# A new order for the head of a decoder step: normalization, transposes, splits, first weights

## The chip, the cores and the metric

The kernel runs on one core of a Trainium2 chip. The metric is the time of one execution in microseconds (us) of device time, as the median of several runs. The engines are PE (TensorE, matmuls and transposes), DVE (VectorE), ACT (ScalarE), POOL (GpSimd) and SP (SyncE, which issues the transfers here). PSUM is the memory that PE writes, in 8 banks; SBUF is the memory that all engines work from.

## The reference

One layer of a decoder trunk for a prompt of 1024 tokens and a sample group of 8 x 8 tokens, which share the weights:

```
h = rmsnorm(x, norm_pre)                      # per token over D_MODEL = 1024
proj = h @ w_in                               # (tokens, 1024) x (1024, 5648)
z, xBC, dt, u, g, gates = split(proj)
branch A: causal conv of width 4 on xBC, SiLU, SSD scan in chunks of 128,
          D skip, SiLU(z) gate, grouped rmsnorm, @ w_branch_a
branch B: trailing means of u (windows 2, 4, 8, 16) minus u, per-group map,
          scale, SiLU(g) gate, @ w_branch_b
merged = sigmoid(gate_a) * A + sigmoid(gate_b) * B
y = x + rmsnorm(merged @ w_out, norm_post)
```

It also returns the convolution, SSD and pool states of both groups. All is float32.

## The kernel before

**Tiles.** The 1088 tokens are nine tiles: tiles 0 to 7 of 128 prompt tokens, tile 8 with the 64 sample tokens. The head normalizes each tile, transposes it (so that channels lie on the partitions) and splits it into a rounded high part `Hhi` and a rest `Hlo` (1024 x 1088 each). Each projection is made of groups of 24 matmuls (`group3`, L142): for one block of 128 output channels and one of three token ranges (256, 384 and 448 columns: tiles 0 and 1, tiles 2 to 4, tiles 5 to 8), eight blocks of input channels times three products (high x high, low x high, high x low). A block of weights (`Slab`) is loaded (L120) and split in the same way into `whi` (a cast on ACT, L93) and `wlo` (a subtraction, L94).

**Order.** Nothing is scheduled automatically: the order in which the program is written is the order of each engine's queue. `main` is the list of matmul groups; a slot is one of its places, and `at_pe(slot, ...)` puts work ahead of that slot's group, `at(slot, ..., key)` behind it, in the order of the keys. The first six groups are the weight blocks 0 and 1 in turn over the three token ranges, so the first group needs tiles 0 and 1 and weight block 0, the second the same tiles and block 1, the third and fourth also tiles 2 to 4, the fifth and sixth also tiles 5 to 8.

**The head's steps.** The head is written as a string of two-character steps, a letter and a tile number; its first part runs ahead of the first group, and the parts behind a bar ahead of the second to fifth group. `loads` is a second such string, for the transfers on SP's queue. The letters:

- R: broadcast half of `norm_pre` to all partitions by a matmul (L1122), and copy it (DVE, L1123).
- N: square and sum of one tile (ACT, L200), then two tiny POOL operations that make the reciprocal root (L182, L183).
- S, D: the tile times root times `norm_pre` (DVE, L209), as one instruction (S) or two halves (D).
- T, U: four transposes each on PE (L223), channels 0 to 511 and 512 to 1023, into one PSUM bank of tag "xb", "pyo" or "pst" by the tile number modulo 3. Each tag has two banks.
- E, F: split of what T or U wrote: the cast to `Hhi` (ACT, L93) and the subtraction to `Hlo` (DVE, L94).
- W, V: split of a weight block, the cast on ACT (L93), the subtraction on POOL (W) or on DVE (V), L94.
- H: a matmul of the identity that nothing reads (L1118). K: seven small POOL operations that make constants (L250 to L258). P: a transpose of the convolution parameters into a "pst" bank (L282) and two copies (L283, L284).
- In the string of transfers: X loads a tile, W a weight block, Q four small parameter tensors.

`hist_dma` loads the convolution history in two transfers (L272) into buffers that the normalized tiles use too (tag "xn", four of them), then the skip vector (L274), `dt_bias` (L277) and `a_log` (L278); `dts.load` follows (L371). ACT takes the exponential of `a_log` (L292) behind the fifth group. The convolution of a finished group runs behind the next groups: a copy out of PSUM and a scaling (ACT, L333 and L341), three taps (DVE, L347).

Of the kernel before, what the change touches and what calls it, by code (L numbers as in the profile page):

```python
# [37 lines left out]
def hybrid_decoder_step(  # L38
# [62 lines left out]
    def at(slot, fn, *args, key=1):  # L101
        post[slot].append((key, len(post[slot]), fn, args))
# [146 lines left out]
    def consts():  # L249
        nc.gpsimd.affine_select(tri, ones, [[1, 128]], ALU.is_ge, 0.0, base=0, channel_multiplier=-1)  # L250
        nc.gpsimd.memset(bones, 0.0)
        b64 = bones[0:64, 0:64].rearrange("p (b t) -> p b t", t=8)
        o64 = ones[0:64, 0:64].rearrange("p (b t) -> p b t", t=8)
        nc.gpsimd.affine_select(b64, o64, [[-8, 8], [0, 8]], ALU.is_ge, 0.0, base=0, channel_multiplier=1)
        nc.gpsimd.affine_select(b64, b64, [[8, 8], [0, 8]], ALU.is_ge, 0.0, base=7, channel_multiplier=-1)
        nc.gpsimd.memset(btri, 0.0)
        nc.gpsimd.tensor_tensor(btri[0:64, 0:64], bones[0:64, 0:64], tri[0:64, 0:64], op=ALU.mult)
        nc.gpsimd.tensor_copy(bm, b64[:, :, 0])  # L258
# [3 lines left out]
    def params_dma():  # L262
        prow = pbox["p"] = mt([72, 128])
        nc.sync.dma_start(prow[0:48], conv_w[0].rearrange("k (t p) -> (k t) p", p=128))
        nc.sync.dma_start(prow[48:60], conv_b[0].rearrange("(t p) -> t p", p=128))
        nc.sync.dma_start(prow[60:68], ssm_norm[0].rearrange("(t p) -> t p", p=128))
        nc.sync.dma_start(prow[68:72], pool_scale[0].rearrange("(t p) -> t p", p=128))
# [12 lines left out]
    def params_T():  # L280
        ps = bank("pst")
        nc.tensor.transpose(ps[:, 0:72], pbox["p"], ident[0:72, 0:72])  # L282
        nc.vector.tensor_scalar(par[:, 0:60], ps[:, 0:60], 0.5, None, op0=ALU.mult)  # L283
        nc.vector.tensor_copy(par[:, 60:72], ps[:, 60:72])  # L284
# [815 lines left out]
    def msplit(m):  # L1100
        mhl[m] = hi, lo = zt((128, LP), F32R), zt((128, LP), F32R)
        for h, l, v in ((hi, lo, mg[m][:, 0:LP]), (ms[m][:, 0:NS], ms[m][:, NS:128], mg[m][:, LP:LT])):
# [8 lines left out]
    nc.sync.dma_start(nrow, norm_pre)  # L1111
    loads = {"W": lambda i: cv[i].slab.dma(raw1[:, 0:1024].rearrange("p (k e) -> p k e", k=8) if i else None),
             "X": load_x, "Q": lambda i: params_dma()}
    for w in "X0 X1 X2 X3 W0 Q0 X4 W1 X5 X6 X7 X8".split():
        loads[w[0]](int(w[1]))

    def H(i):
# [2 lines left out]
    def R(e):  # L1120
# [3 lines left out]

    steps.update({"H": H, "R": R, "W": lambda i: cv[i].slab.conv(nc.gpsimd), "V": lambda i: cv[i].slab.conv(nc.vector),
                  "P": lambda i: params_T(), "K": lambda i: consts()})
    plan = ("R0 N0 R1 H0 N1 D0 H0 T0 U0 S1 N2 H0 S2 T1 N3 U2 T2 F0 W0 S3 E0 U1 E1 H0 T3 H0 U3 N4 F1 D4 W1 | "
            "T4 E2 E3 F2 N5 E4 N6 S5 P0 S6 F3 U4 F4 | "
            "U5 T5 | "
            "T6 N7 F5 K0 U6 D7 T7 E5 | "  # L1130
            "N8 S8 T8 U7 E7 U8 E6 E8 F6 F8 F7")
    for slot, part in enumerate(plan.split("|")):
        for w in part.split():
            fn, n = steps[w[0]], int(w[1])
# [10 lines left out]
    dts = DtStep()  # L1145
    at(3, dts.load, key=5)
    at(6, dts.conv, key=5)
    at(2, hist_dma, key=5)
    at(5, zfree, npre, key=9)

    for i in (8, 10, 2, 3):
# [318 lines left out]
```

## Time and profile before

| what | value |
|---|---|
| median of 3 runs | 913.35 us (912.92 to 913.99) |
| the profiled execution's own time | 914.17 us |
| its span | 912.5 us |
| PE busy | 897.1 us (98%), 5580 matmuls |
| DVE, ACT, POOL busy | 549.1, 346.0, 237.8 us |
| first L142 matmul | 18.43 us from the span's start |

The views in order of time give, for each engine, the start of an instruction in us from the span's start, its length, its line, what it writes and reads, its shape, and in brackets the idle time ahead of it with what ended it. Instructions of one kind that follow each other may stand in one row with their count. A PE row's length reaches to the end of its last matmul, which overlaps the next row; the distance between two starts is what an instruction takes of the engine.

### The profile page before, as it was taken

The page shows a single profiled execution, that of the slowest core. Times are in us where ns is not written, and L with a number is a line of the kernel's source. Part 1 is how long each engine was busy: PE and PEld are TensorE (multiplying, and loading weights), DVE is VectorE, ACT ScalarE, POOL GpSimd, SP SyncE. Part 2 cuts the span into 40 slices and gives each one's busy share as a digit, 9 for nine tenths or more (in the row PEclk, how much of TensorE's full clock was granted, in tenths as well). Part 3 has the DMA queues.
Part 4 walks back from the last instruction along what each step waited for, and adds up shares of the span by engine and source line. Part 5 has one row for each costly group of instructions (what it writes and reads, how often), then busy time and mean ns, then how long its engine had stood idle before and what let it go on. Part 6 is the DMA issues. An engine that isn't in the chain of part 4 may idle for free.

```text
span 912.5 us, 14410 instructions
## 1 busy us (share of the span) xinstructions
PE 897.1 (98%) x5580; PEld 830.8 (91%) x5580; DVE 549.1 (60%) x961; ACT 346.0 (38%) x762; POOL 237.8 (26%) x313
## 2 busy tenths in 40 slices
PE   8999989999999999999999999999999999999997
PEld 6999989999999999998999999999999999988886
DVE  6866797989776675456544353449356526972322
ACT  6645555656375452425343042111333223331111
POOL 6332354656465463121100000000000002510101
PEclk9999999999999999999999999999999999999999
DMA  8011323242335435454311233442121113632222
GB/s 270 8 47 37 85 76 112 68 131 59 107 99 164 120 88 152 116 162 116 93 37 36 35 109 109 148 136 76 54 56 34 45 54 123 228 113 73 92 97 89
DMA packets 112525, 87.97 MB, mean 96 GB/s; under 512 B 10694, under 2 KB 99754, under 8 KB 112457
## 3 DMA queue, kind: packets, MB, share of 16 engines
q1 hardware_dynamic: 112313, 86.92, 32.3%
q8 instruction: 44, 0.72, 0.4%
q14 instruction: 24, 0.20, 0.1%
q10 hardware_dynamic: 144, 0.13, 0.0%
HBM read 69.46 MB, written 17.56 MB: 95 GB/s over the span
## 4 chain that ended last, share of the span: by engine, by line
PE 67%; DVE 2%; DMA 2%; issue 1%; ACT 0%; POOLq 0%; POOL 0%; SPq 0%; DVEq 0%; ACTq 0%
PE m L142 34%; PE pyo L142 16%; PE m L1359 3%; PE pyo L1359 3%; PE xb L1359 3%; PE pst L1359 2%; DMA raw<-in_w_branch_a_dram 1%; PE pyo L568 1%; PE pyo L571 1%; PE xb L694 1%; DVE wlo L94 1%; PE pst L575 1%; PE pst L739 1%; DVE r L347 1%; PE pyo L735 1%
## 5 line engine op out<-in xcount | busy, mean ns | idle before, releaser
L142 PE MATMUL m<-Hhi,whi 128*128 128x384 f32 (+2 forms) x872 | 291.4, 334 | 0.6 <-ACT g L889 0.6
L142 PE MATMUL m<-Hhi,wlo 128*128 128x384 f32 (+2 forms) x872 | 287.1, 329 | 0.0
L142 PE MATMUL m<-Hlo,whi 128*128 128x384 f32 (+2 forms) x872 | 287.0, 329 | 0.0
L142 PEld LDWEIGHTS m<-Hhi,whi 128*128 128x128 f32 x872 | 166.0, 190 | 5.6 <-ACT g L889 1.1
L142 PEld LDWEIGHTS m<-Hlo,whi 128*128 128x128 f32 x872 | 165.9, 190 | 4.3
L142 PEld LDWEIGHTS m<-Hhi,wlo 128*128 128x128 f32 x872 | 165.6, 190 | 4.4
L347 DVE SCALAR_TENSOR_TENSOR r<-r,par,r 128x256 f32<-128x256 f32 (+2 forms) x108 | 97.2, 900 | 2.6
L93 ACT CAST whi<-raw 128x1024 fp32r<-128x1024 f32 (+1 forms) x67 | 59.7, 891 | 99.2 <-PE m L142 35.9
L94 DVE TENSOR_TENSOR wlo<-raw,whi 128x512 fp32r<-128x512 f32 (+1 forms) x46 | 46.7, 1015 | 84.1 <-ACT whi L93 83.9
L94 POOL TENSOR_TENSOR wlo<-raw,whi 128x1024 fp32r<-128x1024 f32 x21 | 51.5, 2452 | 39.9 <-ACT whi L93 34.3
L142 PE MATMUL pyo<-Hhi,whi 128*128 128x448 f32 (+2 forms) x184 | 60.3, 328 | 0.0
L142 PE MATMUL pyo<-Hhi,wlo 128*128 128x448 f32 (+2 forms) x184 | 60.3, 327 | 0.0
L142 PE MATMUL pyo<-Hlo,whi 128*128 128x448 f32 (+2 forms) x184 | 60.2, 327 | 0.0
L142 PE MATMUL m<-z,whi 128*128 128x256 f32 (+2 forms) x217 | 53.3, 327 | 0.0
L142 PE MATMUL pyo<-z,whi 128*128 128x384 f32 (+2 forms) x191 | 48.0, 332 | 1.2 <-ACT whi L93 1.2
L560 POOL TENSOR_TENSOR sa<-sa,cb 128x512 f32<-128x512 f32 x28 | 39.0, 1394 | 6.8 <-ACT sa L556 6.8
L142 PEld LDWEIGHTS m<-z,whi 128*128 128x128 f32 x217 | 38.0, 189 | 1.4
L598 DVE SCALAR_TENSOR_TENSOR z<-z,dsk,se 128x128 f32<-128x128 f32 x56 | 38.5, 727 | 1.0
L142 PE MATMUL m<-z,wlo 128*128 128x256 f32 (+2 forms) x115 | 37.5, 327 | 0.0
L94 POOL TENSOR_TENSOR wolo<-r,wohi 128x512 fp32r<-128x512 f32 x16 | 22.7, 1435 | 56.5 <-ACT wohi L93 53.2
L555 ACT ACTIVATE sa<-sa,acm 128x128 f32<-128x128 f32 x112 | 35.7, 392 | 2.7 <-DMA sa<-dscr 2.7
L341 ACT ACTIVATE r<-r,par 128x256 f32<-128x256 f32 (+2 forms) x36 | 25.1, 698 | 29.7 <-POOL r L329 16.6
(379 smaller groups left out, 1617.6 us busy)
## 6 DMA issues: line engine op xcount, KB each, us to landing
raw<-in_w_in_dram SPq DMA_DIRECT2D x43, 512.0 KB, 4.0
z<-in_x_prompt_dram SPq DMA_DIRECT2D x15, 512.0 KB, 5.2
sa<-dscr SPq DMA_DIRECT2D x28, 256.0 KB, 4.6
z<-spill SPq DMA_DIRECT2D x11, 544.0 KB, 5.4
raw<-in_w_branch_a_dram SPq DMA_DIRECT2D x16, 256.0 KB, 2.8
r<-in_w_out_dram SPq DMA_DIRECT2D x16, 256.0 KB, 4.4
se<-dscr SPq DMA_DIRECT2D x56, 64.0 KB, 4.0
out_dram<-q SPq DMA_DIRECT2D x14, 256.0 KB, 2.1
```

Source lines behind the costliest of these rows:

```text
L93: nc.scalar.copy(hi, src)
L94: (eng or nc.vector).tensor_tensor(lo, src, hi.bitcast(F32), op=ALU.subtract)
L142: nc.tensor.matmul(ps[:, 0:b - a], slab.w(k, p), rhs(k, p)[:, a:b], start=k == 0 and p == 0, stop=k == slab.kn - 1 and p == 2)
L341: nc.scalar.activation(A, R[:, 0:w], AF.Identity, bias=cb(i), scale=cw(0, i))
L347: nc.vector.scalar_tensor_tensor(A, R[:, k:k + w], cw(k, i), A, op0=ALU.mult, op1=ALU.add)
L555: nc.scalar.activation(A[:, h], A[:, h], AF.Relu, bias=acm[:, self.c, hh:hh + 1], scale=-1.0)
L560: nc.gpsimd.tensor_tensor(A, A, CBs[self.c, self.g].unsqueeze(1).to_broadcast([128, 4, 128]), op=ALU.mult)
L568: nc.tensor.matmul(py[64 * q:64 * q + 64, 128 * i:128 * i + 128], x0[:, 2 * i + q], A[:, 2 * i + q], start=True, stop=True)
L571: nc.tensor.matmul(py[:, 256 + 128 * i:384 + 128 * i], hs[:, 128 * i:128 * i + 128], Ct[self.g][:, self.cols], start=True, stop=True)
L575: nc.tensor.matmul(self.ps[:, 0:256], B[:, a], self.xx[:, b].rearrange("p h q -> p (h q)"), start=i == 0, stop=i == 2)
L598: nc.vector.scalar_tensor_tensor(xv, xv, dsk[:, j:j + 1], self.E[:, i] if self.c else py[:, 128 * i:128 * i + 128], op0=ALU.mult, op1=ALU.add)
L1359: nc.tensor.matmul(box["ps"][:, 0:b - a], lh, rh[k][:, a:b], start=kk == 0 and i == 0, stop=kk == 7 and rh is Wlo)
```

## The change

The two strings are written anew, and `hist_dma` moves from behind the third group to behind the fourth, ahead of `dts.load`. In the new string the first weight block is split by V0 (subtraction on DVE) where it was W0 (on POOL); K0 and P0 stand ahead of the first group, where K0 stood ahead of the fourth and P0 ahead of the second; W1 stands ahead of the second group; E0 stands ahead of N2; the scalings of tiles 5 to 8 are halves throughout; X4 is loaded ahead of Q0.

```diff
--- before.py
+++ after.py
@@ -1111,7 +1111,7 @@
     nc.sync.dma_start(nrow, norm_pre)
     loads = {"W": lambda i: cv[i].slab.dma(raw1[:, 0:1024].rearrange("p (k e) -> p k e", k=8) if i else None),
              "X": load_x, "Q": lambda i: params_dma()}
-    for w in "X0 X1 X2 X3 W0 Q0 X4 W1 X5 X6 X7 X8".split():
+    for w in "X0 X1 X2 X3 W0 X4 Q0 W1 X5 X6 X7 X8".split():
         loads[w[0]](int(w[1]))
 
     def H(i):
@@ -1124,11 +1124,10 @@
 
     steps.update({"H": H, "R": R, "W": lambda i: cv[i].slab.conv(nc.gpsimd), "V": lambda i: cv[i].slab.conv(nc.vector),
                   "P": lambda i: params_T(), "K": lambda i: consts()})
-    plan = ("R0 N0 R1 H0 N1 D0 H0 T0 U0 S1 N2 H0 S2 T1 N3 U2 T2 F0 W0 S3 E0 U1 E1 H0 T3 H0 U3 N4 F1 D4 W1 | "
-            "T4 E2 E3 F2 N5 E4 N6 S5 P0 S6 F3 U4 F4 | "
-            "U5 T5 | "
-            "T6 N7 F5 K0 U6 D7 T7 E5 | "
-            "N8 S8 T8 U7 E7 U8 E6 E8 F6 F8 F7")
+    plan = ("N0 R1 R0 N1 D0 T0 E0 N2 H0 U0 S1 H0 U1 F0 T1 S2 H0 T2 N3 S3 H0 F1 H0 K0 V0 E1 N4 D4 U3 U2 T3 F2 F3 P0 | "
+            "U4 W1 E2 E3 N5 F4 D5 T4 E4 N6 | "
+            "D6 N7 T5 N8 | "
+            "D7 D8 U5 T7 T6 U7 U6 E5 T8 F5 E6 U8 F6 E8 E7 F8 F7")
     for slot, part in enumerate(plan.split("|")):
         for w in part.split():
             fn, n = steps[w[0]], int(w[1])
@@ -1145,7 +1144,7 @@
     dts = DtStep()
     at(3, dts.load, key=5)
     at(6, dts.conv, key=5)
-    at(2, hist_dma, key=5)
+    at(3, hist_dma, key=4.5)
     at(5, zfree, npre, key=9)
 
     for i in (8, 10, 2, 3):
```

PE ahead of the first group (main bank `m0`), before: `xb_43` and `xb_45` are T3 and U3, the `m0` rows of L1118 are H.

```order
L1118 MATMUL m0_42_229<-ident_77 128x128
L223 MATMUL xb_43_231<-ident_77,xn_36_199 128x128 x4
L1118 MATMUL m0_44_236<-ident_77 128x128
L223 MATMUL xb_45_238<-ident_77,xn_36_199 128x128 x4
L142 MATMUL m0_51_257<-Hhi_85,whi_39_215 128x256
L142 MATMUL m0_51_257<-Hlo_86,whi_39_215 128x256
L142 MATMUL m0_51_257<-Hhi_85,wlo_40_216 128x256
```

And now: `pst_35` is T2, `xb_46` U3, `pst_47` U2, `xb_48` T3, `pst_49` P0.

```order
L223 MATMUL pst_35_206<-ident_77,xn_28_177 128x128 x4
L1118 MATMUL m0_39_218<-ident_77 128x128
L1118 MATMUL m0_40_222<-ident_77 128x128
L223 MATMUL xb_46_245<-ident_77,xn_38_213 128x128 x4
L223 MATMUL pst_47_250<-ident_77,xn_28_177 128x128 x4
L223 MATMUL xb_48_255<-ident_77,xn_38_213 128x128 x4
L282 MATMUL pst_49_264<-ident_77,m_12_134 128x72
L142 MATMUL m0_50_268<-Hhi_85,whi_41_231 128x256
L142 MATMUL m0_50_268<-Hlo_86,whi_41_231 128x256
L142 MATMUL m0_50_268<-Hhi_85,wlo_42_232 128x256
```

P0 stood behind the first group, between the two halves of tile 4; now the first group stands behind it.

DVE from the scaling of tile 1 on, before (the number behind `xn` and the PSUM tag tells tiles apart: `xn_25`, `xn_31`, `xn_36`, `xn_48` are tiles 1 to 4; `xb_28` is F0, `xb_27` E0, `pyo_33` E1, `pyo_41` F1, `pst_38` F2).

```order
L209 SCALAR_TENSOR_TENSOR xn_25_164<-z_7_124,t_24_163,z_1_99 128x1024
L209 SCALAR_TENSOR_TENSOR xn_31_185<-z_8_126,t_30_184,z_1_99 128x1024
L94 TENSOR_TENSOR Hlo_86<-xb_28_177,Hhi_85 128x4x128
L209 SCALAR_TENSOR_TENSOR xn_36_199<-z_9_128,t_35_198,z_1_99 128x1024
L94 TENSOR_TENSOR Hlo_86<-xb_27_172,Hhi_85 128x4x128
L94 TENSOR_TENSOR Hlo_86<-pyo_33_192,Hhi_85 128x4x128
L94 TENSOR_TENSOR Hlo_86<-pyo_41_222,Hhi_85 128x4x128
L209 SCALAR_TENSOR_TENSOR xn_48_245<-z_12_137,t_47_244,z_1_99 128x512 x2
L94 TENSOR_TENSOR Hlo_86<-pst_38_208,Hhi_85 128x4x128
```

And now: `xn_24`, `xn_28`, `xn_38`, `xn_45` are tiles 1 to 4, `xb_30` is F0, `pyo_32` F1, `wlo_42` V0, `pyo_33` E1, `pst_47` F2, `xb_46` F3.

```order
L209 SCALAR_TENSOR_TENSOR xn_24_162<-z_7_124,t_23_161,z_1_99 128x1024
L94 TENSOR_TENSOR Hlo_86<-xb_30_183,Hhi_85 128x4x128
L209 SCALAR_TENSOR_TENSOR xn_28_177<-z_8_126,t_27_176,z_1_99 128x1024
L209 SCALAR_TENSOR_TENSOR xn_38_213<-z_9_128,t_37_212,z_1_99 128x1024
L94 TENSOR_TENSOR Hlo_86<-pyo_32_191,Hhi_85 128x4x128
L94 TENSOR_TENSOR wlo_42_232<-raw_10_130,whi_41_231 128x1024
L94 TENSOR_TENSOR Hlo_86<-pyo_33_198,Hhi_85 128x4x128
L209 SCALAR_TENSOR_TENSOR xn_45_239<-z_11_132,t_44_238,z_1_99 128x512 x2
L94 TENSOR_TENSOR Hlo_86<-pst_47_250,Hhi_85 128x4x128
L94 TENSOR_TENSOR Hlo_86<-xb_46_245,Hhi_85 128x4x128
```

The subtraction of the first weight block is new on DVE, behind F1, and the scaling of tile 4 (`xn_45`) now stands between E1 and F2.

POOL from the root of tile 3 on, before: `wlo_40` is W0, `t_47` the root of tile 4, `wlo_50` W1.

```order
L182 TENSOR_SCALAR t_35_198<-t_34_197 128x1
L183 TENSOR_TENSOR t_35_198<-t_35_198,half_95 128x1
L94 TENSOR_TENSOR wlo_40_216<-raw_10_130,whi_39_215 128x1024
L182 TENSOR_SCALAR t_47_244<-t_46_243 128x1
L183 TENSOR_TENSOR t_47_244<-t_47_244,half_95 128x1
L94 TENSOR_TENSOR wlo_50_254<-z_5_120,whi_49_253 128x1024
```

And now: `t_37` is the root of tile 3, `t_44` that of tile 4, `wlo_54` W1.

```order
L182 TENSOR_SCALAR t_37_212<-t_36_211 128x1
L183 TENSOR_TENSOR t_37_212<-t_37_212,half_95 128x1
L250 AFFINE_SELECT tri_100<-ones_97 128x128
L251 MEMSET bones_102 128x128
L254 AFFINE_SELECT bones_102<-ones_97 64x64
L255 AFFINE_SELECT bones_102<-bones_102 64x64
L256 MEMSET btri_101 128x128
L257 TENSOR_TENSOR btri_101<-bones_102,tri_100 64x64
L258 COPY bm_103<-bones_102 64x8
L182 TENSOR_SCALAR t_44_238<-t_43_237 128x1
L183 TENSOR_TENSOR t_44_238<-t_44_238,half_95 128x1
L94 TENSOR_TENSOR wlo_54_301<-z_5_120,whi_53_300 128x1024
```

W0's subtraction is gone from behind tile 3's root, and the seven operations of K0 stand in its place, ahead of tile 4's.

## Rows read from the trace of the kernel before

**Rows 1.** The page's part on the chain that ended last: its share by engine.

```profile
PE 67%; DVE 2%; DMA 2%; issue 1%; ACT 0%; POOLq 0%; POOL 0%; SPq 0%; DVEq 0%; ACTq 0%
```

**Rows 2.** PE in order of time, 12 to 44 us: start, length, engine, line, instruction, [idle before].

```profile
12.23 1.97 PE L223 MATMUL pst<-ident,xn 128*128 128x128 f32 x8 [0.89 <-DVE xn L209]
...
16.41 1.09 PE L223 MATMUL xb<-ident,xn 128*128 128x128 f32 x4 [0.93 <-DVE xn L209]
...
18.43 0.56 PE L142 MATMUL m<-Hhi,whi 128*128 128x256 f32 x1
...
19.00 0.41 PE L142 MATMUL m<-Hhi,wlo 128*128 128x256 f32 x1
19.21 0.41 PE L142 MATMUL m<-Hhi,whi 128*128 128x256 f32 x1
...
21.95 0.60 PE L223 MATMUL pyo<-ident,xn 128*128 128x128 f32 x4
...
22.81 0.36 PE L142 MATMUL m<-Hhi,whi 128*128 128x256 f32 x1
...
25.77 1.03 PE L223 MATMUL pst<-ident,xn 128*128 128x128 f32 x8
26.56 0.42 PE L142 MATMUL m<-Hhi,whi 128*128 128x384 f32 x1
...
30.80 1.04 PE L223 MATMUL xb<-ident,xn 128*128 128x128 f32 x8
...
36.80 0.46 PE L223 MATMUL pst<-ident,xn 64*128 64x64 f32 x4 [0.34 <-DVE xn L209]
...
38.17 0.48 PE L142 MATMUL m<-Hhi,whi 128*128 128x448 f32 x1
...
43.24 0.91 PE L290 MATMUL pst<-ident,xn 24*128 24x24 f32 x12
```

**Rows 3.** DVE in order of time, 5 to 30 us.

```profile
7.02 1.41 DVE L209 SCALAR_TENSOR_TENSOR xn<-z,t,z 128x512 f32<-128x512 f32 x2
8.89 1.28 DVE L209 SCALAR_TENSOR_TENSOR xn<-z,t,z 128x1024 f32<-128x1024 f32 x1 [0.45 <-POOL t L183]
...
12.89 3.37 DVE L209 SCALAR_TENSOR_TENSOR xn<-z,t,z 128x1024 f32<-128x1024 f32 x1
...
16.79 1.27 DVE L94 TENSOR_TENSOR Hlo<-pyo,Hhi 128x512 fp32r<-128x512 f32 x2
...
28.20 1.52 DVE L347 SCALAR_TENSOR_TENSOR r<-r,par,r 128x256 f32<-128x256 f32 x3
```

**Rows 4.** POOL in order of time, 5 to 33 us.

```profile
6.16 0.19 POOL L182 TENSOR_SCALAR t<-t 128x1 f32<-128x1 f32 x1 [4.61 <-ACT xn L200]
...
8.94 1.28 POOL L182 TENSOR_SCALAR t<-t 128x1 f32<-128x1 f32 x1
...
12.82 2.36 POOL L94 TENSOR_TENSOR wlo<-raw,whi 128x1024 fp32r<-128x1024 f32 x1
...
29.57 0.30 POOL L250 TENSOR_SCALAR_AFFINE_SELECT tri<-ones 128x128 f32<-128x128 f32 x1
...
31.77 0.19 POOL L258 COPY bm<-bones 64x8 f32<-64x8 f32 x1
```

**Rows 5.** ACT in order of time, 4 to 46 us.

```profile
4.93 1.06 ACT L200 ACTIVATE xn<-z 128x1024 f32<-128x1024 f32 x1 [2.85 <-DMA z<-in_x_prompt_dram]
...
12.09 0.59 ACT L93 CAST Hhi<-pyo 128x512 fp32r<-128x512 f32 x1
...
44.10 0.21 ACT L292 ACTIVATE m<-m 128x16 f32<-128x16 f32 x1
```

**Rows 6.** Line L94, one kind of instruction: count, shortest, middle and longest in ns, forms.

```profile
L94 DVE TENSOR_TENSOR wlo<-raw,whi x46: 681/1212/1785, 355.5 to 800.2; 128x512 fp32r<-128x512 f32 x24, 128x1024 fp32r<-128x1024 f32 x22
```

**Rows 7.** The issues on SP's queue in order of time, 16 to 46 us.

```profile
23.50 1.35 SPq L274 DMA_DIRECT2D dsk<-in_d_skip_dram  x2
```

**Rows 8.** DMA issues of the first 40 us: count, KB each, median us to landing.

```profile
dsk<-in_d_skip_dram SPq DMA_DIRECT2D x2, 2.0 KB, 9.7
```


## Prediction

> **What bounds the kernel now.** I read the chain of waits first, then the instructions of each engine in order of time over the first 45 us. TensorE (PE) makes up two thirds of the chain [rows 1], and from its first projection matmul on it hardly pauses, so this kernel's time is the moment at which that stream starts plus what PE then does. The stream starts at 18.43 [rows 2]; the change lies ahead of that moment and shortly behind it. The reader is to see three things in the rows.
>
> First, what the start waits for now. T3 (four transposes of tile 3) starts at 16.41 after an idle wait of 0.93 us for VectorE's (DVE's) scaling of tile 3, and the first matmul follows 2.0 us later [rows 2]. That scaling took 3.37 us where the same instruction for tile 1 took 1.28 [rows 3]: it began at 12.89, while GpSimd (POOL) held a 2.36 us subtraction from 12.82 to 15.18 [rows 4], and ended 1.1 us after that. The other way round, POOL's first tiny operation for tile 2 took 1.28 us beside DVE's scaling of tile 1 (8.94 to 10.22, and 8.89 to 10.17) and 0.19 alone [rows 3, 4]. So two instructions that both read two operands or one from SBUF on these engines do not run side by side; whichever starts second waits.
>
> Second, PE's rate. In the first group 256 columns take 0.21 us (19.00 to 19.21), the 1.2 GHz level; the second group's 24 matmuls take 2.96 us (22.81 to 25.77), 0.12 each, the upper level [rows 2]. The first group, 18.43 to 21.95, took 3.52 us: it paid 0.56 us for starting before the rate rose. 3.52 us are about six matmuls at 0.21 and eighteen at 0.12, so it rose near 19.7, some 3 us after PE's last pause, which ended at 16.41.
>
> Third, from 21.95 to the start of the fifth group at 38.17 PE waits once, 0.34 us, for the scaling of tile 8 [rows 2].
>
> **The change, part by part.** *Order of R, and fewer warming matmuls ahead of T0:* both broadcast rows of the norm vector are still copied before the first scaling, so it starts at 7.02 as before [rows 3]. Nothing.
>
> *W0 becomes V0, S3 freed.* The first weight tile's subtraction moves from POOL to DVE. Gain: S3 no longer waits for it. But N2 and N3 now stand behind the casts of E0 and F0 on ScalarE (ACT). T0 can start at 7.7 (half of the 1.41 us from 7.02 [rows 3]); four transposes take about 1.0 (eight took 1.97 [rows 2]), the cast 0.59 [rows 5]: 9.4. N2 starts there, 1.2 us later POOL may begin (4.93 to 6.16 [rows 4, 5]), but by then E0's subtraction (0.60, two of them in 1.27 [rows 3]) has let S1 in at 10.1, and POOL gets through at 11.4, when S1's 1.28 us are over. From POOL's first operation to the scaling are 0.86 us (6.16 to 7.02 [rows 3, 4]), of which 0.2 is done by then: S2 runs 12.1 to 13.4. Tile 3 repeats it: S3 14.1 to 15.4, where it ended at 16.26 before. PE then has twelve transposes left (U3, U2, T3), 3.0 us by the same row: it is through at 18.4 at the latest.
>
> *P0 moves ahead of the first group.* This is what decides. P0 writes a bank of the tag "pst", which has two, and the only one given back by then is U2's, so P0 waits until DVE has finished F2; the matmuls stand behind P0 on PE though they don't need it. DVE does, from 15.4: F1 0.6, V0 1.2 (the middle value of this subtraction on DVE is 1.21 [rows 6]), E1 0.6, which makes 17.8, then the scaling of tile 4 (D4, 1.41 [rows 3]) and F2 (0.68).
>
> *K0 moves ahead of tile 4's reciprocal root on POOL.* The constants took 2.39 us there (29.57 to the end of the operation at 31.77 [rows 4]), hidden then beside the third group. Now they start at 14.1 and have to wait out S3 and V0: I take their end at 17.6. Tile 4's two operations add 0.86: D4 starts at 18.4, not 17.8, and ends at 19.8; F2 at 20.5; P0 and the first group at **20.6**, 2.2 us later than 18.43. Bounds: with no wait for POOL at all DVE's own queue from 9.4 is four scalings' worth (S1, S2, S3 at 1.28 and D4 at 1.41), five subtractions at 0.6, one of them to its end at 0.68, and V0: 9.5 us, so 19.0. If K0 found no gap until V0 is through (17.2), its 2.39, 0.86, 1.41 and 0.68 make 22.6. I take 20.6, since K0's short operations do find gaps and only those that read stand still.
>
> The Trainium skill ("SBUF — State Buffer", Who interferes with whom) states that a VectorE instruction with two SBUF inputs contends with a GpSimd instruction that reads SBUF, the one that starts second waiting for the whole instruction, and not with one that only writes. The rule speaks against K0 at this place: by it K0's two memsets pass beside S3 and V0 and its five reading operations do not. If the engines did not exclude each other, K0 would end at 16.5, tile 4's roots at 17.4, D4 would start behind E1 at 17.8 and the group at 20.0, a sum of +1.0 in place of +1.6. By the rule the trace agrees (3.37 us against 1.28).
>
> *The first group.* By my times PE works from 11.5 to 18.4 with no pause over 0.2 us, longer than the stretch after which the rate rose in the profile, then pauses for some 2 us. I take the group at the upper rate: 2.96 us, ending at 23.6 against 21.95, **1.6 us later**. At the lower rate 24 matmuls at 0.21 take 5.0 (the first rival below).
>
> *Transposes of tiles 4 to 8.* W1 now follows its cast, its 2.36 us on POOL run beside DVE's subtractions out of PSUM and end before the first group does. From the end of that group, DVE owes F4 (after U4 0.6 and a cast 0.59), D5, E4, D6, the three taps (1.52 [rows 3]), D7, D8 and E5 before T8 gets a bank: 0.6+0.6+0.6+1.4+0.6+1.4+1.5+1.4+1.4+0.7 = 10.2, and 0.6 for the roots of tiles 6 and 8: 10.8. PE's own work up to there is 0.8 + 2.96 + 0.4 + 4.24 + 2.0 = 10.4 (transposes 0.4 per four, 25.77 to 26.56; the 384-column group 26.56 to 30.80 [rows 2]). T8 waits some 0.5, the eighth tile's second half 0.2 more; before, it waited 0.34 and the turns around it cost 0.3. Zero, with 0.5 either way.
>
> *History rows, moved one slot.* Their two loads now wait for U5 and U7, the latter some 10.2 us after the first group's end, and everything behind them on the DMA queue goes with them: the two loads of the skip vector from 23.50 [rows 7] to about 34.2. Those take 1.35 us to issue [rows 7] and 9.7 to land [rows 8], so a_log behind them lands at 45.3 or a little later; ACT reads it at 44.10 before [rows 5], 45.7 now. That may cost ACT some tenths, which PE does not see while it works on the sixth group, 448 columns wide like the fifth, which took 5 us (38.17 to 43.24 [rows 2]). Nothing; without that cover it would add all that is late.
>
> **Sum.** 2.2 later, 0.56 saved in the first group: **+1.6 us**. The profiled execution took 914.17 with a span of 912.5; it would take 915.8. It lies 0.82 above the median of the three runs, 913.35, from which I predict 913.35 + 1.6 = **915.0**. A measurement of this kernel can tell about 0.2%, 1.83 us, from no change, so +1.6 lies just inside, and its own range, 0.6 to 2.6 (the start 19.6 to 21.6), on both sides of that line.
>
> **Rivals.** *The first group runs at the lower rate.* PE idles 2 us or more before it. For it: transposes and idle time are all that precede. Against: in the profile the rate rose near 19.7, after 2 us of transposes and only 1.3 us of the group's matmuls. It decides if the rate has not risen by 20.6 or has fallen again: 5.0 us instead of 2.96, +3.7, **917.1**, slower. The skill ("TensorE: Matmul & The Clock Gate", Part 4: PE-mode transpose) says that transposes do not count as busy for the clock in the same way; by that the group would start at the lower rate. The first group's 3.52 us, with the rise 1.3 us after its start, speaks against its strict form.
>
> *POOL is never late.* If K0 slips into gaps, DVE's queue alone sets the start, 19.0; with 2.96 the group ends at 21.95, as before: **913.4**, the same.
>
> *F2 is done when PE gets to P0.* Then PE's order alone counts and the freed S3 pays: with the transposes at the upper rate (0.4 per four) from 15.4 the first group starts at 16.7 and ends at 19.7, 2.3 us sooner: **911.1**, faster. It needs F2 off DVE by 16.7, 2.3 us before even the bound of 19.0. For it speaks only that 2.1 us of S3's wait really go.
>
> *The constants behind the history rows land late.* From 5 us of lateness on ACT's evacuation of the fifth group holds up the seventh. At 7 us, 2 us on top of the 1.6: **917.0**. The landing time of 9.7 us speaks against it.
>
> **Chances.** The sum 0.45, lower rate 0.21, POOL never late 0.20, F2 in time 0.09, late constants 0.05. Faster by over 0.2%: 0.07 (most of the fourth). Within: 0.27 of the first, all of the third, the rest of the fourth: 0.49. Slower: 0.18 of the first and the two slow ones: 0.44. The range, 912.4 to 917.4, takes in the third case, both bounds of the start (19.0 and 22.6, the latter +3.6) and the lower rate, and leaves out the fast case and a longer lateness.
>
> **What would show it.** In the changed profile S3 should take 1.28 us and end near 15.4; K0's reading operations should be stretched beside S3 and V0; P0 should show an idle wait of about 2 us for F2's subtraction (a row L94 on DVE); the first L142 matmul should start near 20.6 with 0.12 us per matmul. A start at or before 18.4 or 0.21 us spacing through the whole group would prove me wrong, and so would a wait on PE at T8 of over 1 us.

## The result and the profile after

The changed kernel takes **919.67 us** (median of 6 runs, 917.35 to 920.10) against 913.13 for the kernel before (6 runs beside it, 911.95 to 915.26): ratio **1.0063**, 95% interval 1.0050 to 1.0075. The ratio is 5.75 us on 913.13; the medians themselves lie 6.54 apart. The forecast was 915.0, with 917.4 as the upper end: slower than forecast, by the time and by the range. Timed once more later, it stood at 917.38, which is the end of that range (ratio 1.0041, 1.0022 to 1.0060). The profiled execution took 919.84 us, its span 918.1 against 912.5. Executions of one kernel differ by some us, together with PE's granted clock over the whole span (917.35 us at 0.997 of full speed, 920.10 at 0.993).

PE of the changed kernel in order of time (columns as in [rows 2]):

```profile
13.93 1.06 PE L223 MATMUL pst<-ident,xn 128*128 128x128 f32 x4
...
16.52 0.60 PE L223 MATMUL pst<-ident,xn 128*128 128x128 f32 x4
16.96 0.60 PE L223 MATMUL xb<-ident,xn 128*128 128x128 f32 x4
22.86 0.38 PE L282 MATMUL pst<-ident,m 72*128 72x72 f32 x1 [5.30 <-DVE Hlo L94]
22.99 0.56 PE L142 MATMUL m<-Hhi,whi 128*128 128x256 f32 x1
23.35 0.41 PE L142 MATMUL m<-Hlo,whi 128*128 128x256 f32 x1
23.56 0.41 PE L142 MATMUL m<-Hhi,wlo 128*128 128x256 f32 x1
...
26.82 0.28 PE L142 MATMUL m<-Hhi,whi 128*128 128x256 f32 x1
26.94 0.28 PE L142 MATMUL m<-Hlo,whi 128*128 128x256 f32 x1
...
27.53 1.03 PE L223 MATMUL pyo<-ident,xn 128*128 128x128 f32 x8
...
48.51 0.92 PE L290 MATMUL pst<-ident,xn 24*128 24x24 f32 x12
```

The first group starts at 22.99, not 18.43, and ends at 27.53 (where the transposes of tile 4 start), not 21.95 [rows 2]: 5.58 us late. The history's transposes (L290), where the head is over, start at 48.51, not 43.24: 5.27 late, of the 5.67 us between the two profiled executions. So nearly the whole loss is made ahead of 27.53, in two parts: the start is 4.56 later, and the group's 24 matmuls take 4.54 us where they took 3.52, 1.02 more. P0's row says what ended the wait of 5.30: the subtraction F2 on DVE.

DVE, to be held against [rows 3]:

```profile
14.41 1.30 DVE L209 SCALAR_TENSOR_TENSOR xn<-z,t,z 128x1024 f32<-128x1024 f32 x1 [0.72 <-POOL t L183]
...
16.23 1.21 DVE L94 TENSOR_TENSOR wlo<-raw,whi 128x1024 fp32r<-128x1024 f32 x1
...
18.70 3.51 DVE L209 SCALAR_TENSOR_TENSOR xn<-z,t,z 128x512 f32<-128x512 f32 x2 [0.66 <-POOL t L183]
22.13 0.68 DVE L94 TENSOR_TENSOR Hlo<-pst,Hhi 128x512 fp32r<-128x512 f32 x1
```

And POOL [rows 4]:

```profile
14.85 1.00 POOL L254 TENSOR_SCALAR_AFFINE_SELECT bones<-ones 64x64 f32<-64x64 f32 x1
...
16.43 1.18 POOL L257 TENSOR_TENSOR btri<-bones,tri 64x64 f32<-64x64 f32 x1
17.56 0.18 POOL L258 COPY bm<-bones 64x8 f32<-64x8 f32 x1
...
19.26 2.40 POOL L94 TENSOR_TENSOR wlo<-z,whi 128x1024 fp32r<-128x1024 f32 x1 [0.59 <-ACT whi L93]
```

The scaling of tile 3, 3.37 us before, takes 1.30 and ends at 15.7. K0's reading operations are stretched beside S3 and V0 (L254 took 1.00 us and L257 1.18, where they took 0.29 and 0.47 before), as forecast. The row that was not forecast is DVE's at 18.70: D4, two halves of 0.7 us each, takes **3.51** where tile 0's pair takes 1.41 [rows 3]. POOL's row at 19.26 shows why: W1's subtraction stood ready when the first half ended (18.70 + 0.7 = 19.4) and ran to 21.66; D4 ended 0.55 us behind that, at 22.21. The second half had to wait for the whole of it.

D4 was late in the kernel before, too, in rows that stand in none of the groups: its two halves took 2.50 us, beside W1's subtraction, which held POOL from 16.91 to 19.27.

```profile
17.98 2.50 DVE L209 SCALAR_TENSOR_TENSOR xn<-z,t,z 128x512 f32<-128x512 f32 x2
```

```profile
16.91 2.36 POOL L94 TENSOR_TENSOR wlo<-z,whi 128x1024 fp32r<-128x1024 f32 x1
```

There the first group did not stand behind F2, and PE did not wait for D4.

PE's granted clock by stretch (start and end, length, PE busy, instructions, granted share of 2.4 GHz, DMA's busy share and GB/s):

```profile
15.00:18.00 3.00, 2.56 (x16) 1.00 0.97 340
18.00:20.50 2.50, 0.00 (x0) 0.86 0.74 200
20.50:23.00 2.50, 0.14 (x2) 0.50 0.06 17
23.00:26.00 3.00, 3.00 (x15) 0.50 0.00 0
26.00:28.00 2.00, 2.00 (x17) 0.85 0.00 0
```

PE stops behind T3, near 17.5. The grant (the clock that the chip allows PE) falls to a half, the 1.2 GHz level, while it stands, and comes back only when the group's matmuls have run for some time: 0.21 us apart at 23.35, 0.12 at 26.82.

### The profile page after: what moved, and what is told of

Its sections match the earlier page's. It is cut to its first block, busy times and chain, and to the rows that moved or that the text cites. A ratio compares the mean times of both kernels' runs of the same rounds, so it can differ in the third digit from the quotient of the medians.

```text
span 918.1 us, 14410 instructions
## 1 busy us (share of the span) xinstructions
PE 896.2 (98%) x5580; PEld 831.2 (91%) x5580; DVE 548.1 (60%) x965; ACT 345.9 (38%) x762; POOL 235.8 (26%) x312
## 3 DMA queue, kind: packets, MB, share of 16 engines
HBM read 69.46 MB, written 17.56 MB: 95 GB/s over the span
## 4 chain that ended last, share of the span: by engine, by line
PE 69%; DMA 1%; DVE 1%; issue 1%; ACT 0%; POOLq 0%; POOL 0%; ACTq 0%
PE m L142 35%; PE pyo L142 17%; PE m L1358 3%; PE pyo L1358 3%; PE xb L1358 2%; PE pst L1358 2%; DMA raw<-in_w_branch_a_dram 1%; PE pyo L568 1%; PE pyo L571 1%; PE xb L694 1%; PE pst L575 1%; PE pst L739 1%; DVE r L347 1%; PE pyo L735 1%; PE pst L823 0%
## 5 line engine op out<-in xcount | busy, mean ns | idle before, releaser
L94 DVE TENSOR_TENSOR wlo<-raw,whi 128x512 fp32r<-128x512 f32 (+1 forms) x47 | 46.8, 995 | 80.7 <-ACT whi L93 80.7
L94 POOL TENSOR_TENSOR wlo<-raw,whi 128x1024 fp32r<-128x1024 f32 x20 | 49.0, 2452 | 38.3 <-ACT whi L93 34.4
L94 POOL TENSOR_TENSOR wolo<-r,wohi 128x512 fp32r<-128x512 f32 x16 | 22.8, 1446 | 56.4 <-ACT wohi L93 56.4
L142 PEld LDWEIGHTS pyo<-Hlo,whi 128*128 128x128 f32 x184 | 34.8, 189 | 1.4
```

Of the source, the lines that this page charges most:

```text
L94: (eng or nc.vector).tensor_tensor(lo, src, hi.bitcast(F32), op=ALU.subtract)
L142: nc.tensor.matmul(ps[:, 0:b - a], slab.w(k, p), rhs(k, p)[:, a:b], start=k == 0 and p == 0, stop=k == slab.kn - 1 and p == 2)
```

## The experiments

Times are medians. "Start" and "end" are those of the first group in the profiled execution, "L290" the start of the history's transposes, all in us.

| kernel | median us | ratio to before (95%) | start | end | L290 |
|---|---|---|---|---|---|
| before | 913.13 | 1 | 18.43 | 21.95 | 43.24 |
| changed | 919.67 | 1.0063 (1.0050 to 1.0075) | 22.99 | 27.53 | 48.51 |
| changed, again | 917.38 | 1.0041 (1.0022 to 1.0060) | 22.75 | 26.91 | 47.89 |
| tile 4 in one piece | 916.33 | 1.0020 (1.0008 to 1.0031) | 20.50 | 24.95 | 45.94 |
| W1 later | 917.02 | 1.0043 (1.0023 to 1.0063) | 20.82 | 23.78 | 44.77 |
| K0 behind | 916.15 | 1.0014 (1.0002 to 1.0026) | 19.86 | 22.82 | 43.88 |
| P0 behind | 914.15 | 0.9994 (0.9982 to 1.0007) | 17.70 | 21.00 | 42.51 |
| P0 and K0 behind | 912.04 | 0.9985 (0.9974 to 0.9996) | 16.99 | 20.82 | 41.85 |
| 26 H in the pause | 917.54 | 1.0033 (1.0022 to 1.0044) | 24.14 | 27.09 | 48.09 |
| 20 H in the pause | 916.54 | 1.0025 (1.0012 to 1.0038) | 22.76 | 25.71 | 46.72 |
| 12 H, W1 later | 914.51 | 0.9998 (0.9983 to 1.0012) | 21.10 | 24.04 | 45.04 |
| before with V0 | 910.73 | 0.9979 (0.9967 to 0.9992) | 16.75 | 19.71 | 41.36 |
| before with V0, S4 | 911.56 | 0.9982 (0.9971 to 0.9993) | 16.24 | 19.20 | 40.75 |
| a third order | 910.98 | 0.9975 (0.9964 to 0.9987) | 15.29 | 19.74 | 41.09 |

Each batch of experiments had its own runs of the kernel before beside it (medians 913.37 to 914.49); the ratios are to those. The grant also falls behind the head, in some executions: in the profiled ones near 126 us in the kernel before and near 532 us in the changed one (0.50 in both, read in stretches of 2 us), and nowhere with P0 behind. So a ratio is read with its interval, and the trace of one execution shows the mechanism, not the mean.

**The changed kernel again.**

> The changed kernel itself, timed beside the others. Theory A: as in its first profile, D4 is cut by W1's subtraction where that is ready before the second half starts; there the two instants lay 0.13 us apart (first half done 19.39, W1 ready 19.26), so in some executions the cut may be missing and the time up to 2.3 us lower. Expected: 918 to 920, ratio 1.005 to 1.007.

1.0041 is below the expected 1.005 to 1.007, with an interval that reaches 1.0060; one execution of the seven took 914.55. In the profiled one D4 was cut again (3.51 us from 18.46).

**Tile 4 in one piece.**

```diff
-... K0 V0 E1 N4 D4 U3 U2 T3 F2 F3 P0 |
+... K0 V0 E1 N4 S4 U3 U2 T3 F2 F3 P0 |
```

> The changed kernel with the scaling of tile 4 as one DVE instruction (S4) in place of two halves (D4). Theory A (the first group waits for F2; 2.1 of the 5.6 us come from W1's subtraction on POOL, 2.40 us from 19.26, which gets in between the two halves of D4): D4 takes 1.3 to 1.4 us from 18.7 and ends near 20.0, W1's subtraction starts behind it, F2's subtraction ends near 20.7, the first group starts near 20.8 in place of 22.99; with its 4.54 us as in the changed kernel the time falls by 2.2 us (about 917.4, +4.3 on before), with the upper rate (2.96 us) by 3.8 (about 915.9). Rival B (the place of P0 and the cut do not matter, the history rows' move does): no change, 919.7.

DVE, POOL and PE of this kernel:

```profile
18.47 1.28 DVE L209 SCALAR_TENSOR_TENSOR xn<-z,t,z 128x1024 f32<-128x1024 f32 x1 [0.66 <-POOL t L183]
```

```profile
18.75 3.24 POOL L94 TENSOR_TENSOR wlo<-z,whi 128x1024 fp32r<-128x1024 f32 x1 [0.32 <-ACT whi L93]
```

```profile
20.41 0.28 PE L282 MATMUL pst<-ident,m 72*128 72x72 f32 x1 [3.35 <-DVE Hlo L94]
20.50 0.36 PE L142 MATMUL m<-Hhi,whi 128*128 128x256 f32 x1
...
24.95 0.82 PE L223 MATMUL pyo<-ident,xn 128*128 128x128 f32 x6
```

W1's subtraction was ready at 18.75, found DVE at work and waited (3.24 us with its wait). The start is 2.49 us earlier. The rate still fell: the group takes 4.45 us. The ratio is 1.0020 where the changed kernel has 1.0063 and 1.0041: 2 to 4 us less, as theory A has it. Its interval is clear of the first of these, not of the second.

**P0 behind the first group.**

```diff
-... U3 U2 T3 F2 F3 P0 | U4 W1 E2 E3 N5 F4 D5 T4 E4 N6 |
+... U3 U2 T3 F2 F3 | U4 W1 E2 E3 N5 F4 D5 P0 T4 E4 N6 |
```

> The changed kernel with P0 moved behind the first group (ahead of T4), nothing else. Theory A: the first group no longer waits for F2; it waits for E1's subtraction (18.0) and T3 and starts near 18.2, at the upper rate or soon in it (transposes to 17.4 ahead of it), ends near 21.2 to 21.8; then U4 waits for the second half of tile 4's scaling, which W1 still cuts (22.2), so the second group starts near 23 as against 28.3: 4.5 to 5.3 us less than the changed kernel, 914.4 to 915.2, i.e. +1.3 to +2 on before. Rival B (history rows): 919.7. Rival C (the first group runs at the lower rate whatever comes ahead of it, since transposes do not raise it): 24 x 0.21 = 5 us from 18.2, ends 23.2, then no wait at U4: about 3.8 us less than the changed kernel.

DVE, POOL and PE:

```profile
18.75 1.42 DVE L209 SCALAR_TENSOR_TENSOR xn<-z,t,z 128x512 f32<-128x512 f32 x2 [0.66 <-POOL t L183]
```

```profile
19.64 2.77 POOL L94 TENSOR_TENSOR wlo<-z,whi 128x1024 fp32r<-128x1024 f32 x1 [0.93 <-ACT whi L93]
```

```profile
17.70 0.36 PE L142 MATMUL m<-Hhi,whi 128*128 128x256 f32 x1
```

The start is 17.70, no wait stands ahead of the group, and the whole loss is gone (ratio 0.9994). The history rows and K0 stand where the change put them, so rival B is out. Theory A was wrong on a detail: U4 did not wait, since D4 was not cut here (1.42 us from 18.75). PE's rate rose later in this execution (T3 starts at 17.34, not 16.96), F2's cast came later with it, and W1 was ready at 19.64, after the second half had begun. The cut (W1's subtraction between D4's halves) hangs on some tenths.

**K0 behind F5.** K0 moves from ahead of V0 to behind F5, nothing else.

> The changed kernel with the constants K0 moved to the part ahead of the fifth group, behind F5. Theory A: the roots of tile 4 come earlier on POOL (by up to 1 us), D4 then follows E1 at 18.0, its second half starts before W1's subtraction is ready at 19.26, and is not cut: D4 18.0 to 19.4, F2's subtraction to 20.1, first group at 20.2 in place of 22.99: 2.8 us less than the changed kernel with its group of 4.54 us, 4.4 less with the upper rate (about 915.3 to 916.9). If the second half still starts behind 19.26, it is cut again and the gain is under 0.8 us. Rival B: 919.7.

DVE and PE:

```profile
17.72 1.41 DVE L209 SCALAR_TENSOR_TENSOR xn<-z,t,z 128x512 f32<-128x512 f32 x2
```

```profile
19.78 0.28 PE L282 MATMUL pst<-ident,m 72*128 72x72 f32 x1 [2.73 <-DVE Hlo L94]
...
22.82 1.03 PE L223 MATMUL pyo<-ident,xn 128*128 128x128 f32 x8
```

D4 follows E1 at 17.72 in place of 18.70 and is not cut (1.41 us): K0 costs the scaling 1 us, and here it also decides the cut. P0 waits 2.73 us, and the group behind that pause runs at the upper rate throughout: 19.86 to 22.82, the 2.96 us of the forecast. The median, 916.15, is as expected, but 3 us above this execution (913.17, the fastest of twelve). That the rate fell in others is likely and not shown.

**H in the pause.** 26 H stand between T3 and P0.

> The changed kernel with 26 more matmuls of the identity that nothing reads (H) on PE between T3 and P0, so that PE works through most of its wait for F2. Theory A (the rate fell because PE stood idle for 5.3 us): the first group starts near 23.0 as in the changed kernel, and its 24 matmuls stand 0.12 us apart and take 2.96 us in place of 4.54: 1.6 us less, 918.1. Rival C (PE's rate is low there for what was done ahead, whether it idled or not): 4.5 us again, 919.7.

PE of this kernel:

```profile
17.05 7.17 PE L1118 MATMUL m<-ident 128*128 128x128 f32 x52
24.05 0.23 PE L282 MATMUL pst<-ident,m 72*128 72x72 f32 x1
24.14 0.36 PE L142 MATMUL m<-Hhi,whi 128*128 128x256 f32 x1
...
27.09 0.38 PE L223 MATMUL pyo<-ident,xn 128*128 128x128 f32 x2
```

The 26 H (52 matmuls) outlast the wait for F2, whose subtraction ends at 22.75, by 1.3 us, and the group takes 2.95 us: the idle time had lowered the rate, not the transposes ahead of it. Since the H delay the start, L290 is only 0.42 us ahead of the changed kernel's. The time falls by 2 to 3 us against the first measurement of the changed kernel, more than this trace accounts for, and by nothing clear against the second. So the trace shows the rate here, and the time does not price it.

**W1 later.**

```diff
-U4 W1 E2 E3 N5 F4 D5 T4 E4 N6 |
+U4 E2 E3 W1 N5 F4 D5 T4 E4 N6 |
```

> The changed kernel with W1 behind E3 in place of behind U4 (two casts of 0.5 us each go ahead of W1's cast on ACT), D4 left in two halves. Theory A (it is W1's subtraction that cuts D4, by being ready between the halves): W1 is ready near 20.2 in place of 19.26, D4's second half has then begun, D4 takes 1.4 us in place of 3.51, F2's subtraction ends near 20.7 and the first group starts near 20.8 in place of 22.99; time as with the scaling in one piece, 2 to 4 us less than the changed kernel. Rival (two halves as such cost 3.5 us at that place): start at 23.0, no change.

DVE, POOL and PE:

```profile
18.67 1.42 DVE L209 SCALAR_TENSOR_TENSOR xn<-z,t,z 128x512 f32<-128x512 f32 x2 [0.67 <-POOL t L183]
```

```profile
19.92 2.41 POOL L94 TENSOR_TENSOR wlo<-z,whi 128x1024 fp32r<-128x1024 f32 x1 [1.29 <-ACT whi L93]
```

```profile
20.74 0.28 PE L282 MATMUL pst<-ident,m 72*128 72x72 f32 x1 [3.48 <-DVE Hlo L94]
```

The halves are still two; D4 takes 1.42 us from 18.67, since W1 came at 19.92. So it is W1, not the halves. The start is 2.2 us earlier. The time did not show it: 1.0043 (1.0023 to 1.0063) against 1.0041 for the changed kernel's second measurement, in another batch. In this profiled execution the rate held through the pause of 3.48 us, and in the kernel with tile 4 in one piece it fell behind one of 3.35, so the rate seems to differ from execution to execution there, which would cover the difference. Hence a pair of kernels in which PE has next to no pause.

**The cut with the rate held, the pair.** "12 H, W1 later" and "20 H in the pause" both fill PE up to P0 (all but 0.23 us); one has W1 behind E3, the other where the change put it.

> The changed kernel with W1 behind E3 (no cut of D4) and 12 H between T3 and P0, so that PE has next to no pause ahead of the first group and its rate cannot be the difference. Theory A: D4 1.4 us, first group from 20.8 at 0.12 us per matmul, ends near 23.8, 1.9 us later than before; 2.1 us less than the same with the cut (20 H, W1 in its place), measured beside it: ratio about 1.001 to 1.002.

> The changed kernel with 20 H between T3 and P0, W1 in its place. Theory A: D4 is cut (3.5 us), the first group starts near 22.9 at 0.12 us per matmul and ends near 25.9 in place of 27.53, 4.0 us later than before: 1 to 2 us less than the changed kernel, 2.1 us more than the kernel with W1 later and 12 H: ratio about 1.003 to 1.004. If both come out alike, the cut is not worth its 2.1 us in the time.

With 12 H and W1 later, DVE and PE:

```profile
18.64 1.41 DVE L209 SCALAR_TENSOR_TENSOR xn<-z,t,z 128x512 f32<-128x512 f32 x2 [0.67 <-POOL t L183]
```

```profile
17.83 3.34 PE L1118 MATMUL m<-ident 128*128 128x128 f32 x24
21.01 0.23 PE L282 MATMUL pst<-ident,m 72*128 72x72 f32 x1
21.10 0.35 PE L142 MATMUL m<-Hhi,whi 128*128 128x256 f32 x1
...
24.04 1.03 PE L223 MATMUL pyo<-ident,xn 128*128 128x128 f32 x8
```

With 20 H and W1 in its place:

```profile
18.48 3.52 DVE L209 SCALAR_TENSOR_TENSOR xn<-z,t,z 128x512 f32<-128x512 f32 x2 [0.67 <-POOL t L183]
```

```profile
16.90 5.53 PE L1118 MATMUL m<-ident 128*128 128x128 f32 x40
22.66 0.28 PE L282 MATMUL pst<-ident,m 72*128 72x72 f32 x1 [0.23 <-DVE Hlo L94]
22.76 0.36 PE L142 MATMUL m<-Hhi,whi 128*128 128x256 f32 x1
...
25.71 0.49 PE L223 MATMUL pyo<-ident,xn 128*128 128x128 f32 x3
```

Both groups run at the upper rate. The one start is 1.66 us ahead of the other (the 12 H run some 0.3 us longer than the wait for F2), and the medians are 914.51 and 916.54, **2.03 us apart**, for 2.1 us of D4. Both ratios lie about 0.1% below what was expected; it is their difference that the pair is for. The cut is settled in the trace and in the time. The second kernel differs from the changed one by its H alone: its group ends 1.82 us sooner (25.71 for 27.53), 1.59 of it from the rate (2.95 us for 4.54).

**P0 and K0 behind.** Both edits above together.

> The changed kernel with both P0 (ahead of T4) and K0 (behind F5) moved back behind the first group. Theory A: the first group starts at 17.7 as with P0 moved alone (it waits for T3, E1 and PE's own transposes, not for tile 4); D4 follows E1 at 17.7 to 18.0 and cannot be cut, so U4 behind the first group never waits: within 0.5 us of the kernel with P0 moved alone (ratio to before 0.999), and never up to 2 us above it as that one could be where the cut occurs.

The median is 912.04, the ratio 0.9985. D4 starts at 17.83 and takes 1.40 us, and nothing waits at U4. The first matmul starts at 16.99, the second waits 0.62 us for E1's subtraction. The changed order without these two moves is not worse than the order before.

**V0 alone, in the kernel before.**

```diff
-... N3 U2 T2 F0 W0 S3 E0 U1 E1 H0 T3 H0 U3 N4 F1 D4 W1 |
+... N3 U2 T2 F0 V0 S3 E0 U1 E1 H0 T3 H0 U3 N4 F1 D4 W1 |
```

> The kernel before with the first weight block's subtraction on DVE (V0 for W0) and nothing else. Theory A (the freed scaling S3 is the part of the change that helps, and the other parts cost): S3 takes 1.3 us from 12.9 in place of 3.37, but V0's 1.2 us now stand ahead of it on DVE, so S3 ends near 15.4 in place of 16.26, T3 starts near 15.5, the first group near 17.6 in place of 18.43; later groups partly wait for the same DVE work: 0.3 to 0.9 us less than before, which the measurement hardly tells from no change. If instead V0's work on DVE costs as much as POOL's lock did, no change in the start.

DVE and PE of this kernel:

```profile
13.71 1.28 DVE L209 SCALAR_TENSOR_TENSOR xn<-z,t,z 128x1024 f32<-128x1024 f32 x1
...
16.70 3.50 DVE L209 SCALAR_TENSOR_TENSOR xn<-z,t,z 128x512 f32<-128x512 f32 x2
```

```profile
15.15 1.07 PE L223 MATMUL xb<-ident,xn 128*128 128x128 f32 x4
...
16.75 0.36 PE L142 MATMUL m<-Hhi,whi 128*128 128x256 f32 x1
...
19.71 0.60 PE L223 MATMUL pyo<-ident,xn 128*128 128x128 f32 x4
```

S3 takes 1.28 us and T3 starts at 15.15, not 16.41 [rows 2]. PE loses its pause there, the rate is up before the group starts, and it runs 16.75 to 19.71: 2.96 in place of 3.52. Both add up, 2.24 us at the group's end, more than the 0.3 to 0.9 expected, which had left the rate out. The median is 910.73, the ratio 0.9979 (0.9967 to 0.9992): **0.2% faster than the kernel before, by one letter**. D4 is cut here too (3.50 us), but P0, which stands behind the group, waits only 0.55 us for F2.

**V0 and S4, in the kernel before.**

> The kernel before with V0 for W0 and tile 4's scaling in one piece. There too, with V0 alone, D4 was cut (3.50 us from 16.70, W1's subtraction from 16.58), but only P0, behind the first group, waited for it, 0.55 us. Theory A: S4 starts behind or ahead of W1's subtraction as a whole; if ahead, F2 ends 2 us sooner, P0's 0.55 us go and the rest stays: 0.3 to 0.6 us less than V0 alone (ratio 0.9975); if W1 is first again, no change (0.998).

W1 was first again (15.43, for 2.40 us) and S4 took 2.15. The ratio is 0.9982: no difference from V0 alone that the measurement shows.

**A third order.** From the changed kernel, with a new string:

```diff
+R1 R0 N0 D0 N1 N2 H0 N3 T0 U0 D1 S2 T1 E0 U1 H0 D3 F0 T2 N4 U2 E1 W0 T3 N5 E2 F1 S4 E3 U3 |
+U4 V1 S5 T4 P0 F2 N7 D7 E4 F3 |
+N8 U5 F4 S8 N6 F5 T5 D6 E5 |
+T8 T6 U7 E8 U8 U6 F7 T7 K0 F8 F6 E6 E7
```

> A third order of the same steps: N2 and N3 ahead of the casts of E0 and F0; W0 on POOL behind U2, where DVE has only subtractions out of PSUM and halves of tile 3 beside it; two H fewer ahead of the first group; K0 behind T7; V1 on DVE. Estimate from the rows: scalings of tiles 1 to 3 follow each other from 8.9 without POOL's or ACT's delay (four at 1.3 to 1.4 us and subtractions of 0.6), so that T3 and U3 are through near 16 and the first group starts near 16.5, 1.9 us sooner than before; the first matmuls run at the lower rate (at most 1 us given back). Expected 1 to 2.5 us less than before (912 to 913.5 where before measures 914.5). A rival (DVE's total work before the third group is what bounds, not the start): no change.

The median is 910.98, the ratio 0.9975 (0.9964 to 0.9987). The group starts at 15.29, where 16.5 was expected, but its third matmul waits 1.16 us for W0's subtraction on POOL, and it ends at 19.74, as with V0 alone. The two don't differ by more than the measurement tells.

The history's move has no run of its own. ACT's reading of a_log waited 1.89 us in the changed kernel,

```profile
51.34 0.22 ACT L292 ACTIVATE m<-m 128x16 f32<-128x16 f32 x1 [1.89 <-DMA m<-in_a_log_dram]
```

and 1.81 with P0 behind, where no time was lost.

## Why the prediction was wrong

- **S3 freed**: right. It ran from 14.41 for 1.30 us (forecast 14.1 to 15.4).
- **K0 on POOL**: right. Its last operation starts at 17.56 (forecast end 17.6), the reading ones wait out S3 and V0, and D4 starts at 18.70 (forecast 18.4).
- **P0 waits for F2**: right, and it is the part that decides; with P0 behind, the loss goes (0.9994).
- **The step that failed**: "W1 now follows its cast, its 2.36 us on POOL run beside DVE's subtractions out of PSUM and end before the first group does." They did end before the group did (21.66), but they ran in the middle of D4, which reads SBUF twice. I had counted D4 as one piece of 1.41 us; it is two instructions, with a gap that POOL can enter. The term was mis-sized by 2.1 us (3.51 against 1.41). Without the cut the first group starts at 20.50, where 20.6 was forecast. This mechanism stood in none of my rivals, though it is that of S3 in [rows 3, 4], which I had read out as the reason for the wait before. The 1.41 was tile 0's, with no subtraction on POOL beside it; D4's own row before, 2.50 us beside W1, already spoke against it.
- **The rate in the first group**, the other term that was off: 2.96 forecast, 4.54 measured, 1.6 us more. The lower rate was a rival, at 0.21, with the right reason (the pause) and the wrong independence: I gave it a start of 20.6, as if the length of the wait had no part in it. A pause of 2.73 us left the rate alone (K0 behind), and one of 5.30 did not. T3 also ended near 17.5, where 18.4 was the latest forecast, which alone lengthens the pause by 0.9. Of all the pauses ahead of the first group the two longest (5.30 and 5.58 us, both of the changed kernel) had the lower rate behind them, so what lengthens the wait and the rate belong in one case: +2.2, +2.4 and +1.0 (22.99 for 20.6, 4.54 for 3.52) give the 5.58.
- **Transposes as the cause of the lower rate**, the first rival's other reason: the Trainium skill ("TensorE: Matmul & The Clock Gate", Part 4: PE-mode transpose) says that transposes don't count as busy in the same way. Here the rate rose in a stretch of transposes and a few H (U2 and T3 0.44 us apart, from 16.52), and it held through the H in the pause. So idle time lowered it; that transposes count for less is not borne out here, though no run had transposes alone.
- **Transposes of tiles 4 to 8 at zero**: right within 0.5. From the group's end to L290 are 20.98 us, before 21.29, and PE waits for none of them.
- **Late constants**: they were late (the skip vector's loads were issued at 38.24, not 34.2, since the group ended at 27.53, not 23.6), and PE did not wait for it, as forecast. ACT waited 1.89 us, where some tenths were forecast.

## What to carry to other kernels

Cost each instruction, not each step: a pair of halves on DVE can be entered by a GpSimd instruction that stands ready, and then the second half waits for the whole of that one. Before an operation is put ahead of PE's main stream, ask what gives back the bank it needs; anything else that delays that comes with it. And a long wait on PE can be paid twice: once as time, once in the rate of what follows.

## What the runs showed of the hardware

- Between DVE's scaling and POOL's subtraction one instruction is the unit of exclusion. The 2.40 us of W1 between D4's halves turned 1.41 us into 3.51, and with tile 4 in one piece the same W1 waited and took 3.24. The Trainium skill ("SBUF — State Buffer", Who interferes with whom) says that issue order decides who blocks; the pair of runs with W1 moved agrees, worth 2.03 us of the whole.
- PE's rate does not follow from a pause's length alone: the group ran at the upper rate behind 2.73 and 3.48 us, and mostly at the lower one behind 3.35 (granted 0.60 in 20.5 to 23.0) and 5.30 (granted 0.50), each in one profiled execution. In the changed kernel's second profile PE stopped near 17.0, half a us sooner than in the first, but the grant still read 1.00 up to 22 us, and 0.50 only from 23 to 25.
- The granted clock reads 1.00 from 12 to 18 us in the changed kernel, while four transposes took 1.06 us at 13.93 and 0.60 at 16.52: the column shows the later fall but not the lower rate at the start. There the spacing of the matmuls has to be read.
